# A transformer trunk on one core: G loads queued behind the weights, and part of the output added in memory by accumulating transfers

## The chip, the core and the metric

The kernel runs on one core of a Trainium2 chip. A core has five engines with instruction streams of their own: TensorE (PE, matmuls, with weight loads shown apart as PEld), VectorE (DVE), ScalarE (ACT), GpSimd (POOL) and SyncE (SP). Each stream is executed in order. SP, ACT and POOL also issue DMAs; those of SP and ACT go through hardware queues, those of POOL through a software queue, and all are carried out by the same 16 DMA engines. PE accumulates in PSUM; the other engines and the DMAs work on SBUF, the on-chip memory of 128 partitions. "Memory" below is the chip's large off-chip memory, in which inputs, outputs and spilled intermediates lie.

The metric is the device time of one execution in microseconds (us), as a median over runs.

## The reference

One layer over 512 tokens of width 2048, all in float32:

```python
h = rms_norm(x, g0)
P = h @ w_in                       # 11 column blocks for four groups of heads
mixed = concat[A, B, C, D] @ w_out # stick-breaking attention, differential attention, RG-LRU, gated conv
x = x + rms_norm(mixed, g1)        # this sum is x1
h = rms_norm(x, g2)
u = causal_dwconv(h @ ffn_w_up, ffn_conv_w)
g, up = split(u)
x = x + rms_norm((gelu(g) * up) @ ffn_w_down, g3)
```

An RMS norm multiplies each token by the inverse root of its mean square and each channel by a gain. The product gelu(g) * up is called G here; it has 4096 channels, 32 blocks of 128. The last line is where the change does most: the output is x1 plus the scaled result of the down projection.

## The kernel before

**Layout.** Channels lie on the partitions and the 512 tokens along the free axis. A matrix product is done in float32 precision by three passes on split operands: every operand is kept as a rounded high part and a remainder (hi and lo). ScalarE makes hi by a cast and VectorE makes lo by a subtraction (`split`, lines 175 to 182; for weights lines 99 and 100 in `chunk`, 1008 and 1009 in `operand`).

**Order.** PE's order is the order of the program text (`manual_schedule`, line 53). The other engines' orders are made by a planner, which picks among the instructions that are ready by priority: the place in the text, with loads and splits of weights far ahead (`high_priority`). `issue_after(ins)` puts an instruction behind another on the same engine's stream; it is an order only and no wait for the other to finish. Work that accompanies the matmuls is hung on a counter: `at(block, fn)` runs a function when the counter `clock[0]` reaches a step, and the loop of `group` counts four steps for each chunk of weights (`tick`, lines 111 to 114).

**First norm and residual.** After the out projection, for each half of the tokens, `residual(hf)` (line 828) scales the result and adds it onto x: half of it by VectorE (line 842), half by accumulating DMAs from POOL into SBUF (line 838). Then `squares` makes the squares (ScalarE, line 853) and their sum (VectorE, line 855) and stores x1 to memory (`x1_d`, line 859). `norm2` (line 861) sums over the partitions with four matmul passes (line 866), makes the inverse root and splits the normalized h. It is hung 40 steps behind `residual` (line 845).

**Up projection.** `seven` (line 1023) does seven block products in place of eight for each unit of 128 channels (a scheme of Strassen's kind); it needs sums of weight blocks, of which some are made by accumulating DMAs from POOL (line 1018). Each unit ends in a convolution (lines 948 and 950), and `glu` (line 957) stores one block of G to memory (`g_d`, line 959).

**Down projection.** G comes back from memory in pairs of blocks. `load_pair` (line 1128) takes a tile of the pool `ystage` (two tiles) and issues two loads of 256 KB from SP; `load_g` (line 1134) splits two pairs into a tile of four blocks. Blocks 0 to 3 (line 1142) and 20 to 31 (lines 1213 to 1215) are used by plain products, blocks 4 to 19 by the scheme of seven (`load_build`, line 1175, `down_unit`, line 1194). The plain products of blocks 20 to 31 come last: three groups of 512 output channels with all tokens, and the fourth once for each half of the tokens (lines 1243 to 1246).

**Last norm and output.** `SumSq` (line 789) takes the squares of the 16 output blocks. POOL adds the squares up in order, except for the last `direct` ones, which PE takes as further terms of its sum over the partitions (lines 811 and 812). `rstd_of` (line 184) makes the inverse root in six small instructions (lines 188 to 194) with two temporary tiles `f1`. `finish(hf)` (line 1229) does the rest for a half: for q = 0 to 3 it loads 4 blocks of x1 (512 KB, line 1235), multiplies the result by the inverse root (line 1239), adds x1 (line 1240) and stores pieces of two blocks (256 KB, line 1241), in turn from SP and ACT. The x1 of q = 0 has a pool of its own with one tile (`x1p`), that of q = 1 to 3 uses the two tiles of `ystage`. For the second half this whole sequence lies behind the last matmul of the kernel.

Of the kernel before, what the change touches and what calls it, by code (L numbers as in the profile page):

```python
# [9 lines left out]
F32 = mybir.dt.float32  # L10
F32R = mybir.dt.float32r
AF = mybir.ActivationFunctionType
ALU = mybir.AluOpType
# [3 lines left out]
P = 128  # L17
S = 512
# [30 lines left out]
def trunk(ctx: ExitStack, tc: tile.TileContext, xT, params, consts, wgate, w_in, w_out, w_up0, w_up, w_dn, w_dns, out):  # L49
    nc = tc.nc  # L50
    V, A, G, T = nc.vector, nc.scalar, nc.gpsimd, nc.tensor
# [9 lines left out]
    def mm_tile():  # L61
        return mm.tile([P, S], F32, name="mm")
# [23 lines left out]
    w_split, w_load = [], []  # L86
# [18 lines left out]
    clock = [0]  # L105

    def at(block, fn):
        assert block >= clock[0], (block, clock[0])
        beside.setdefault(block, []).append(fn)
# [62 lines left out]
    def repeated(t, n):  # L172
        return t.unsqueeze(1).broadcast_to([P, n, t.shape[-1]])

    def split(src, hi, lo, scale=None):
        if scale is None:
            A.copy(out=hi, in_=src)
            V.tensor_tensor(out=lo, in0=src, in1=hi.bitcast(F32), op=ALU.subtract)
        else:
            A.activation(out=hi, in_=src, func=AF.Copy, scale=scale)  # L180
            V.scalar_tensor_tensor(out=lo, in0=src, scalar=scale, in1=hi.bitcast(F32),
                                   op0=ALU.mult, op1=ALU.subtract)

    def rstd_of(ss, n, dst, tmp):

        w = dst.shape[-1]
        v = tmp()[:, 0:w]
        V.tensor_scalar(out=v, in0=ss, scalar1=-0.5 / n, scalar2=-0.5 * EPS, op0=ALU.mult, op1=ALU.add)
        y = tmp()[:, 0:w]
        A.activation(out=y, in_=ss, func=AF.Ln, scale=1.0 / n, bias=eps)  # L190
        exp = A.activation(out=y, in_=y, func=AF.Exp, scale=-0.5)
        V.tensor_tensor(out=v, in0=v, in1=y, op=ALU.mult)
        V.tensor_tensor(out=v, in0=v, in1=y, op=ALU.mult)
        V.scalar_tensor_tensor(out=dst, in0=v, scalar=1.5, in1=y, op0=ALU.add, op1=ALU.mult)
        return exp
# [23 lines left out]
    x1_d = [dram.tile([P, 2, 4, S // 2], F32, name=f"x1_d{q}") for q in range(4)]  # L219
    g_d = [dram.tile([P, S], F32, name=f"g_d{k}") for k in range(FF // P)]  # L220
# [4 lines left out]
    with ExitStack() as ph:  # L225
# [145 lines left out]
        for i in range(2):  # L371
            V.tensor_tensor(out=lmp[:, i * 64:(i + 1) * 64], in0=par[:, dl + 128 * i:dl + 128 * i + 64],
                            in1=par[:, dl + 128 * i + 64:dl + 128 * i + 128], op=ALU.mult)
# [247 lines left out]
        ys, vs = {}, []  # L621
# [150 lines left out]
    with ExitStack() as ph:  # L772
        wide = ph.enter_context(tc.tile_pool(name="wide", bufs=2))
        ystage = ph.enter_context(tc.tile_pool(name="ystage", bufs=2))
# [6 lines left out]
        ph2 = norm_ph.enter_context(tc.tile_pool(name="ph2", bufs=1))  # L781
# [2 lines left out]
            return t2p.tile([P, S], dt, name="f2")  # L784

        def t1(dt=F32):
            return ph2.tile([P, S // 2], dt, name="f1", bufs=3)

        class SumSq:

# [37 lines left out]
        def residual(hf):  # L828

            ts = HALVES[hf]  # L830
            ss1[hf].rstd(rstd1[:, ts])
            acc = ph2.tile([P, 2, S // 2], F32, name="s2")
            for q in range(4):
                for i in range(2):
                    m = mg[q][hf][:, 2 * i:2 * i + 2]
                    V.tensor_tensor(out=m, in0=m, in1=repeated(rstd1[:, ts], 2), op=ALU.mult)
                if q < 2:
                    G.dma_start(out=xs[q][hf], in_=mg[q][hf], accum_op=ALU.add)
            for q in range(2, 4):
                for i in range(2):  # L840
                    m, x = (t[q][hf][:, 2 * i:2 * i + 2] for t in (mg, xs))
                    V.tensor_tensor(out=x, in0=x, in1=m, op=ALU.add)
            for q in range(4):
                at(clock[0] + 20 + 3 * q, lambda q=q: squares(hf, q, acc))
            at(clock[0] + 40, lambda: norm2(hf, acc))

        def squares(hf, q, acc):

            with tc.issue_after(w_split[-1].ins):
                for i in range(2):  # L850
                    n = 2 * q + i
                    sq = acc if n == 0 else t2().rearrange("p (k t) -> p k t", k=2)
                    A.activation(out=sq, in_=xs[q][hf][:, 2 * i:2 * i + 2], func=AF.Square)
                    if n > 0:
                        V.tensor_tensor(out=acc, in0=acc, in1=sq, op=ALU.add)
                for i in range(4):
                    A.activation(out=mg[q][hf][:, i], in_=xs[q][hf][:, i], func=AF.Copy, scale=gain(2, 4 * q + i))
            with tc.issue_after(w_load[-1].ins):
                nc.sync.dma_start(out=x1_d[q][:, hf], in_=xs[q][hf])

        def norm2(hf, acc):

            ts = HALVES[hf]
            ps = mm_tile()[:, 0:S // 2]
            for i in range(2):
                T.matmul(ps, lhsT=ones, rhs=acc[:, i], start=i == 0, stop=i == 1)
            with tc.high_priority(offset=AHEAD):
                rstd_of(ps, D, rstd2[:, ts], t1)
            for k in range(0, KT, 2):
                ks = slice(k % 4, k % 4 + 2)  # L870
                h = mg[k // 4][hf][:, ks]
                V.tensor_tensor(out=h, in0=h, in1=repeated(rstd2[:, ts], 2), op=ALU.mult)
                split(h, actq[k // 4][:, 0, ks, ts], actq[k // 4][:, 1, ks, ts])
            if hf == 1:
                sums_of_h()
# [9 lines left out]
        def sums_of_h():  # L885


            t1_, t3_ = (wide.tile([P, 2, KT // 2, S // 2], F32R, name="xs") for _ in range(2))
            for i in range(2):
                h11, h12, h22 = mg[i][0], mg[i][1], mg[2 + i][1]  # L890
                ks = slice(4 * i, 4 * i + 4)
                V.tensor_tensor(out=h11, in0=h11, in1=h12, op=ALU.subtract)
                split(h11, t1_[:, 0, ks], t1_[:, 1, ks])
                V.tensor_tensor(out=h12, in0=h22, in1=h12, op=ALU.subtract)
                split(h12, t3_[:, 0, ks], t3_[:, 1, ks])
            for i in range(2):
                t1, h21, h22 = mg[i][0], mg[2 + i][0], mg[2 + i][1]
                V.scalar_tensor_tensor(out=h22, in0=t1, scalar=-1.0, in1=h22, op0=ALU.mult, op1=ALU.subtract)
                V.scalar_tensor_tensor(out=h21, in0=h22, scalar=-1.0, in1=h21, op0=ALU.mult, op1=ALU.subtract)
            t4_ = wide.tile([P, 2, KT // 2, S // 2], F32R, name="mg")  # L900
            for i in range(2):
                split(mg[2 + i][0], t4_[:, 0, 4 * i:4 * i + 4], t4_[:, 1, 4 * i:4 * i + 4])
            for n, t in (("T1", t1_), ("T3", t3_), ("T4", t4_)):
                tops[n] = [t[:, :, k] for k in range(8)]
# [219 lines left out]
        m3 = [m3p.tile([P, 4, S], F32, name=f"m3{q}") for q in range(4)]  # L1124
# [2 lines left out]

        def load_pair(k, pool=None):
            y = (ystage if pool is None else pool).tile([P, 2, S], F32, name="ys")
            for i in range(2):  # L1130
                nc.sync.dma_start(out=y[:, i], in_=g_d[k + i])
            return y

        def load_g(k, t):

            for i in range(0, 4, 2):
                with tc.high_priority(offset=AHEAD):
                    split(load_pair(k + i), t[:, 0, i:i + 2], t[:, 1, i:i + 2])
                for n in range(i, i + 2):
                    g_h[k + n], g_l[k + n] = t[:, 0, n], t[:, 1, n]  # L1140
# [69 lines left out]
        x1p = ph.enter_context(tc.tile_pool(name="x1p", bufs=1))  # L1210
        ph2 = ph.enter_context(tc.tile_pool(name="ph3", bufs=1))
        rstd3 = ph2.tile([P, S], F32, name="rstd3")
        load_g(20, wide.tile([P, 2, 4, S], F32R, name="xs"))
        load_g(24, wide.tile([P, 2, 4, S], F32R, name="xs"))
        load_g(28, act.tile([P, 2, 4, S], F32R, name="a1"))
        ss3 = [SumSq("q3", 3), SumSq("q3", 3)]

        def last_group(g, hfs, ts, pool_tile):
            def evac(u, ps):
# [9 lines left out]
        def finish(hf):  # L1229
            ts = HALVES[hf]  # L1230
            ss3[hf].rstd(rstd3[:, ts])
            for q in range(4):
                x1 = (x1p if q == 0 else ystage).tile([P, 2, S], F32, name="ys")
                x1 = x1.rearrange("p a (b t) -> p (a b) t", b=2)
                nc.sync.dma_start(out=x1, in_=x1_d[q][:, hf])
                for i in range(2):
                    ks = slice(2 * i, 2 * i + 2)
                    t, x = m3[q][:, ks, ts], x1[:, ks]
                    V.tensor_tensor(out=t, in0=t, in1=repeated(rstd3[:, ts], 2), op=ALU.mult)
                    V.tensor_tensor(out=x, in0=t, in1=x, op=ALU.add)  # L1240
                    (nc.scalar if i else nc.sync).dma_start(out=out[hf, 2 * q + i], in_=x)

        for g in range(3):
            last_group(g, (0, 1), ALL, mm_tile if g % 2 == 0 else pa_tile)
# [117 lines left out]
```

## Time and profile before

| | us |
|---|---|
| median of 3 runs | 1788.43 (1787.79 to 1792.69) |
| the profiled execution, its time | 1789.35 |
| the profiled execution, its span (first to last instruction) | 1787.7 |

The span is what the profile's times refer to, counted from its start. The mean TensorE clock granted in this execution was 0.990. The second part of the page cuts the span into 40 slices of 44.7 us; PE's digit is 7 to 9 in all of them but the last, where it is 4. The longest idle time of PE in front of one instruction is 10.1 us (the waits of line 1039), the sum of all its waits that the trace names is about 35 us.

How to read the lines that follow in the next parts: a timeline line has the start, the time from there to the end of the instructions merged in it, engine, line of the kernel, operation, the tile written and the tiles read, shapes and count, and in brackets how long the engine had been idle before and what ended that. SPq, ACTq and POOL lines with DMA_DIRECT2D are issues of DMAs; when the data lands is told by the view of DMAs, whose lines have the engine, count, size of one and the median time from issue to landing. A line of the DMA queues has packets, megabytes, and the share of the 16 engines' time that they took.

### The profile page before, as it was taken

How to read it: one execution, taken by the hardware profiler on the slowest of the kernel's cores; microseconds unless marked ns; L12 is line 12 of the kernel's file. 1: busy time of each engine (PE TensorE's matmuls, PEld its weight loads, DVE VectorE, ACT ScalarE, POOL GpSimd, SP SyncE). 2: the span in 40 equal slices, each digit the busy share in tenths (PEclk: the TensorE clock that was granted, in tenths of full speed). 3: DMA queues.
4: the chain of work that ended last, by engine and by line, in shares of the span. 5: the costliest groups of instructions: out<-in, count | busy, mean ns of one | idle time of the engine just before them, and what ended most of it. 6: DMA issues, size and time to landing. Idle time of an engine off the chain costs nothing.

```text
span 1787.7 us, 25033 instructions
## 1 busy us (share of the span) xinstructions
PE 1730.8 (97%) x9500; PEld 1501.8 (84%) x9500; DVE 1245.1 (70%) x1903; ACT 897.0 (50%) x1335; POOL 162.3 (9%) x230
## 2 busy tenths in 40 slices
PE   8999999999999999999799999999999999999994
PEld 7778788887888889999688888888888878888884
DVE  7885576666666324879788888888878886775336
ACT  6443676655334334767455555555555663334432
POOL 0000011100000111100011111111111001110211
PEclk9999999999999999999899999999999999999997
DMA  7234222242222535775788888888888669876235
GB/s 255 83 100 142 83 77 77 88 143 94 94 93 89 195 107 178 234 223 175 227 212 226 234 232 213 246 230 222 235 230 228 174 205 247 223 191 188 94 122 185
DMA packets 97024, 308.13 MB, mean 172 GB/s; under 512 B 10468, under 2 KB 14820, under 8 KB 96904
## 3 DMA queue, kind: packets, MB, share of 16 engines
q1 hardware_dynamic: 80056, 247.29, 41.8%
q0 software_dynamic: 15696, 57.15, 17.2%
q10 hardware_dynamic: 1152, 2.10, 0.3%
q8 instruction: 74, 1.21, 0.3%
q14 instruction: 46, 0.38, 0.1%
HBM read 265.59 MB, written 21.24 MB: 160 GB/s over the span
## 4 chain that ended last, share of the span: by engine, by line
PE 89%; DMA 4%; DVE 4%; ACT 2%; issue 1%; SPq 0%; DVEq 0%; ACTq 0%; POOLq 0%
PE mm L150 34%; PE mm L1039 25%; PE mm L1044 13%; PE pa L150 5%; PE mm L121 2%; PE mm L122 2%; PE mm L123 2%; PE pa L575 1%; DVE w_lo L100 1%; DMA a<-in_w_dns_dram 1%; DMA ys<-x_d 1%; DMA g_d<-f 1%; PE pa L123 1%; PE pa L121 1%; PE pa L122 1%
## 5 line engine op out<-in xcount | busy, mean ns | idle before, releaser
L100 DVE TENSOR_TENSOR w_lo<-w_raw,w_hi 128x1024 fp32r<-128x1024 f32 (+1 forms) x207 | 253.6, 1225 | 263.5 <-PE mm L150 136.1
L150 PE MATMUL mm<-a,w_hi 128*128 128x512 f32 (+1 forms) x1744 | 371.0, 363 | 2.7 <-DVE t L318 2.1
L99 ACT CAST w_hi<-w_raw 128x1024 fp32r<-128x1024 f32 (+1 forms) x207 | 216.1, 1045 | 293.3 <-PE mm L150 214.9
L150 PEld LDWEIGHTS mm<-a,w_hi 128*128 128x128 f32 x1744 | 296.7, 189 | 53.4 <-DVE t L318 2.6
L1039 PE MATMUL mm<-a,w_hi 128*128 128x512 f32 x1088 | 276.4, 396 | 16.3 <-DVE ub L1106 10.1
L1008 ACT CAST w_hi<-w_raw 128x1024 fp32r<-128x1024 f32 x145 | 152.2, 1050 | 203.5 <-PE mm L1039 175.6
L1039 PEld LDWEIGHTS mm<-a,w_hi 128*128 128x128 f32 x1088 | 197.8, 191 | 52.7 <-DVE ub L1106 10.3
L1009 DVE TENSOR_TENSOR w_lo<-w_raw,w_hi 128x1024 fp32r<-128x1024 f32 x145 | 177.0, 1221 | 36.9 <-ACT w_hi L1008 36.9
L150 PE MATMUL mm<-a,w_lo 128*128 128x512 f32 (+1 forms) x872 | 198.1, 366 | 0.0
L150 PEld LDWEIGHTS mm<-a,w_lo 128*128 128x128 f32 x872 | 147.2, 189 | 24.0 <-issue 1.5
L1044 PEld LDWEIGHTS mm<-a,w_lo 128*128 128x128 f32 x1088 | 150.5, 193 | 11.0
L1044 PE MATMUL mm<-a,w_lo 128*128 128x256 f32 x1088 | 153.5, 284 | 0.0
L1039 PE MATMUL mm<-xs,w_hi 128*128 128x512 f32 x576 | 144.3, 392 | 0.2 <-DVE ub L1106 0.2
L1008 ACT CAST w_hi<-mg 128x1024 fp32r<-128x1024 f32 x84 | 87.7, 1044 | 86.4 <-PE mm L1039 83.0
L1009 DVE TENSOR_TENSOR w_lo<-mg,w_hi 128x1024 fp32r<-128x1024 f32 x84 | 102.5, 1221 | 24.8 <-ACT w_hi L1008 24.8
L1039 PEld LDWEIGHTS mm<-xs,w_hi 128*128 128x128 f32 x576 | 103.6, 189 | 19.0 <-DVE ub L1106 0.4
L1039 PE MATMUL mm<-mg,w_hi 128*128 128x512 f32 x352 | 88.2, 392 | 0.8 <-DVE m L1200 0.8
L1044 PEld LDWEIGHTS mm<-xs,w_lo 128*128 128x128 f32 x576 | 78.6, 190 | 5.6
L1106 DVE TENSOR_TENSOR ub<-ub,mm 128x256 f32<-128x256 f32 x196 | 81.3, 415 | 0.7 <-ACT ub L1103 0.7
L1044 PE MATMUL mm<-xs,w_lo 128*128 128x256 f32 x576 | 80.3, 282 | 0.0
L150 PE MATMUL pa<-a,w_hi 128*128 128x256 f32 (+1 forms) x512 | 72.8, 294 | 2.9 <-ACT w_hi L99 2.9
L1039 PEld LDWEIGHTS mm<-mg,w_hi 128*128 128x128 f32 x352 | 63.3, 189 | 12.3 <-issue 1.0
(267 smaller groups left out, 2556.9 us busy)
## 6 DMA issues: line engine op xcount, KB each, us to landing
w_raw<-in_w_up_dram SPq DMA_DIRECT2D x115, 512.0 KB, 5.1
w_raw<-in_w_in_dram SPq DMA_DIRECT2D x87, 512.0 KB, 3.5
mg<-in_w_up_dram SPq DMA_DIRECT2D x56, 512.0 KB, 3.9
w_raw<-in_w_out_dram SPq DMA_DIRECT2D x48, 512.0 KB, 3.5
w_raw<-in_w_dn_dram SPq DMA_DIRECT2D x38, 512.0 KB, 3.6
w_raw<-mg POOLq DMA_DIRECT2D x28, 512.0 KB, 5.8
mg<-in_w_up_dram POOLq DMA_DIRECT2D x27, 512.0 KB, 7.9
w_raw<-in_w_up_dram POOLq DMA_DIRECT2D x27, 512.0 KB, 9.2
```

The source lines that it names most:

```text
L99: w_split.append(A.copy(out=hi[:, sl], in_=raw[:, sl]))
L100: V.tensor_tensor(out=lo[:, sl], in0=raw[:, sl], in1=hi[:, sl].bitcast(F32), op=ALU.subtract)
L121: T.matmul(ps, lhsT=sh, rhs=mh, start=first, stop=False)
L122: T.matmul(ps, lhsT=sh, rhs=ml, start=False, stop=False)
L123: T.matmul(ps, lhsT=sl, rhs=mh, start=False, stop=last)
L150: T.matmul(pss[u], lhsT=a, rhs=b, start=c == 0 and kk == 0 and not low and i == 0, stop=False)
L575: T.matmul(cum[:, o0:o0 + w], lhsT=stat, rhs=mv, start=n == 0, stop=n == len(todo) - 1)
L1008: w_split.append(A.copy(out=by4(hi), in_=v))
L1009: V.tensor_tensor(out=by4(lo), in0=v, in1=by4(hi).bitcast(F32), op=ALU.subtract)
L1039: T.matmul(ps.rearrange("p (a t) -> p a t", a=2), lhsT=hi[:, k * P:(k + 1) * P], rhs=tops[name][k], start=first and k == 0, stop=False, **kw)
L1044: T.matmul(ps[:, 0:256], lhsT=lo[:, k * P:(k + 1) * P], rhs=tops[name][k][:, 0], start=False, stop=k == 7, **kw)
L1106: V.tensor_tensor(out=t, in0=t, in1=ps[:, 256:512], op=ALU.add)
```

## The change

Four edits:

- `load_pair` issues its two loads behind the last weight load that stands ahead of it in the text (`issue_after(w_load[-1].ins)`).
- For the second half of the tokens, output pieces 0 to 4 of 8 take another way. Five copies from x1 in memory to the output in memory are issued from SP behind the weights of the last unit of the scheme of seven. In `finish(1)` the scaled result of each of these pieces is added onto the output in memory by an accumulating DMA from POOL. They need no x1 in SBUF and no add by VectorE. Pieces 5 to 7, and the whole first half, still load x1, add and store.
- The x1 of q = 0 and of q = 3 now use the tile of `x1p`, q = 1 and q = 2 the two tiles of `ystage`. For the second half only half of q = 2 is loaded, and q = 3.
- The last norm's sums take two squares directly instead of one, with four tiles for squares instead of three; the temporary tiles `f1` go from three to two; `norm2` is hung 43 steps behind `residual` for the first half and 41 for the second, instead of 40.

```diff
         def t1(dt=F32):
-            return ph2.tile([P, S // 2], dt, name="f1", bufs=3)
+            return ph2.tile([P, S // 2], dt, name="f1", bufs=2)
...
-            at(clock[0] + 40, lambda: norm2(hf, acc))
+            at(clock[0] + (43 if hf == 0 else 41), lambda: norm2(hf, acc))
...
             y = (ystage if pool is None else pool).tile([P, 2, S], F32, name="ys")
-            for i in range(2):
-                nc.sync.dma_start(out=y[:, i], in_=g_d[k + i])
+            with tc.issue_after(w_load[-1].ins):
+                for i in range(2):
+                    nc.sync.dma_start(out=y[:, i], in_=g_d[k + i])
             return y
...
-        ss3 = [SumSq("q3", 3), SumSq("q3", 3)]
+
+        IN_OUT = 5
+        with tc.issue_after(w_load[-1].ins):
+            for n in range(IN_OUT):
+                nc.sync.dma_start(out=out[1, n], in_=x1_d[n // 2][:, 1, 2 * (n % 2):2 * (n % 2) + 2])
+        ss3 = [SumSq("q3", 4, 2), SumSq("q3", 4, 2)]
...
         def finish(hf):
             ts = HALVES[hf]
             ss3[hf].rstd(rstd3[:, ts])
-            for q in range(4):
-                x1 = (x1p if q == 0 else ystage).tile([P, 2, S], F32, name="ys")
-                x1 = x1.rearrange("p a (b t) -> p (a b) t", b=2)
-                nc.sync.dma_start(out=x1, in_=x1_d[q][:, hf])
-                for i in range(2):
-                    ks = slice(2 * i, 2 * i + 2)
-                    t, x = m3[q][:, ks, ts], x1[:, ks]
-                    V.tensor_tensor(out=t, in0=t, in1=repeated(rstd3[:, ts], 2), op=ALU.mult)
-                    V.tensor_tensor(out=x, in0=t, in1=x, op=ALU.add)
-                    (nc.scalar if i else nc.sync).dma_start(out=out[hf, 2 * q + i], in_=x)
+            def scaled(n):
+                t = m3[n // 2][:, 2 * (n % 2):2 * (n % 2) + 2, ts]
+                V.tensor_tensor(out=t, in0=t, in1=repeated(rstd3[:, ts], 2), op=ALU.mult)
+                return t
+
+            n = 0
+            while hf == 1 and n < IN_OUT:
+
+                G.dma_start(out=out[hf, n], in_=scaled(n), accum_op=ALU.add)
+                n += 1
+            while n < 8:
+                q, i = n // 2, n % 2
+                if i == 0 or hf == 1 and n == IN_OUT:
+                    x1 = (x1p if q % 3 == 0 else ystage).tile([P, 2, S], F32, name="ys")
+                    x1 = x1.rearrange("p a (b t) -> p (a b) t", b=2)
+                    nc.sync.dma_start(out=x1[:, 2 * i:], in_=x1_d[q][:, hf, 2 * i:])
+                t, x = scaled(n), x1[:, 2 * i:2 * i + 2]
+                V.tensor_tensor(out=x, in0=t, in1=x, op=ALU.add)
+                (nc.scalar if i else nc.sync).dma_start(out=out[hf, n], in_=x)
+                n += 1
```

## The prediction

> **What bounds the kernel now.** I read the page first, then the chain of waits, then the timeline wherever the chain leaves TensorE, because only there can a change of loads, buffers and an output path move the end.
>
> ```profile
> span 1787.7 us, 25033 instructions
> PE 1730.8 (97%) x9500; PEld 1501.8 (84%) x9500; DVE 1245.1 (70%) x1903; ACT 897.0 (50%) x1335; POOL 162.3 (9%) x230
> ...
> q1 hardware_dynamic: 80056, 247.29, 41.8%
> q0 software_dynamic: 15696, 57.15, 17.2%
> ...
> PE 89%; DMA 4%; DVE 4%; ACT 2%; issue 1%; SPq 0%; DVEq 0%; ACTq 0%; POOLq 0%
> ```
>
> TensorE is busy 97% of the span and the chain is PE for 89% of it. The change removes no matmul. It can only win what lies in PE's holes, and in the tail after PE's last matmul. The tail is the largest hole. Its timeline:
>
> ```profile
> 1759.18 0.38 SPq L1235 DMA_DIRECT2D ys<-x_d  x1
> ...
> 1763.63 1.73 POOL L802 TENSOR_TENSOR ss<-ss,q 128x256 f32<-128x256 f32 x2 [0.21 <-ACT q L798]
> ...
> 1765.42 0.70 PE L812 MATMUL pa<-ss,con 128*128 128x256 f32 x2 [1.92 <-POOL ss L802]
> ...
> 1765.95 0.59 PE L812 MATMUL pa<-q,con 128*128 128x256 f32 x2
> 1768.01 0.69 DVE L1240 TENSOR_TENSOR ys<-m,ys 128x512 f32<-128x512 f32 x1 [3.70 <-DMA ys<-x_d]
> 1768.61 0.41 DVE L188 TENSOR_SCALAR f<-pa 128x256 f32<-128x256 f32 x1
> ...
> 1770.93 0.42 DVE L194 SCALAR_TENSOR_TENSOR rstd<-f,f 128x256 f32<-128x256 f32 x1
> 1771.39 1.29 DVE L1239 TENSOR_TENSOR m<-m,rstd 128x512 f32<-128x512 f32 x2
> ...
> 1772.60 1.28 DVE L1240 TENSOR_TENSOR ys<-m,ys 128x512 f32<-128x512 f32 x2
> ...
> 1782.97 1.29 DVE L1240 TENSOR_TENSOR ys<-m,ys 128x512 f32<-128x512 f32 x2 [3.07 <-DMA ys<-x_d]
> ```
>
> PE's last matmul ends at 1766.54, 21.2 us before the end. Two waits for x1 stand in that tail. The first half's last add (L1240) waits for its x1 until 1768.01, and the second half's L188 stands behind it on VectorE, 2.07 us after PE is done. From L188 to the end of rstd (1771.35) is 2.74. Then come 8 multiplies and 8 adds at 0.60 each, with a second wait of 3.07 for the last x1 tile, whose buffer came free late. The last store is issued at 1784.3:
>
> ```profile
> L1241 ACTq DMA_DIRECT2D out_dram<-ys x8: 338/338/377, 1756.9 to 1784.3; - x8
> ```
>
> **The tail after the change.** PE first. One more square per half goes straight to PE (direct 1 to 2). A term costs PE 0.53 (1765.42 to 1765.95), so the first half's sum puts up to 0.53 into the matmul stream. In the second half POOL does one add less (1.73/2 = 0.87), and the sum is done at 1766.54 - 0.87 + 0.53 = 1766.20. Together the end of PE work is 1766.7, level with before.
>
> The first half's last x1 (q = 3) changes its buffer: it now goes into x1p, which is free at 1759.18 (there before loads the second half's first x1). With the 4.6 of such a load (row below) it lands at 1763.8, both adds are over by 1765.2 and L188 follows PE at once, at 1766.8. rstd is done at 1769.5, 1.85 earlier. If that load comes late, the 1.85 shrinks.
>
> Now the output. The 5 accumulating pieces need a multiply and no add on VectorE, and no x1 in SBUF; pieces 5 to 7 keep both. Multiply 0 ends at 1770.2. POOL then issues five DMAs, and the prices of an accumulating DMA are these (window 862 to 868, where that queue was alone, and all of L1018):
>
> ```profile
> q0 software_dynamic: 221, 0.84, 79.1%
> ```
>
> ```profile
> L1018 POOL DMA_DIRECT2D w_raw<-in_w_up_dram x27: 862/865/888, 875.6 to 1396.0; - x27
> ...
> DMA to landing us min/median/max: 4.5/7.8/10.8
> ```
>
> ```profile
> ys<-x_d SPq DMA_DIRECT2D x8, 512.0 KB, 4.6
> ```
>
> ```profile
> out_dram<-ys ACTq DMA_DIRECT2D x1, 256.0 KB, 2.1
> ```
>
> The last row is the last store of all (window 1780 to 1788). Issue is 0.87 each, so the first bytes move at 1771.1 and the fifth issue begins near 1773.9. The rate: 0.84 MB in 79.1% of 6 us is 177 GB/s alone, and 57.15 MB in 17.2% of 1787.7 is 186 GB/s over the whole run (plain transfers: 247.29 MB in 41.8%, 331 GB/s). Five pieces of 262144 bytes are 1.31 MB, 7.05 us at 186. The quickest landing of 512 KB, 4.5, is 0.87 of issue, 2.8 of transfer and 0.8 of rest. So the fifth lands at 1771.1 + 7.05 + 0.8 = 1778.95 if the DMA engines serve nothing else. The three plain stores and one x1 load (1.31 MB, 4.0 us at 331) share the time: 1782.95 at worst. I take the middle, 1781.0. No row has an accumulation whose destination is memory; all of before's go to SBUF. So this is a choice by the nearest rows, and both ends go into the range: 1775.9 (five at the plain 331 GB/s, 4.0) and 1787 (half the rate, with the x1 load beside it).
>
> Nothing is queued behind the five on POOL, whose last own work is the sum of squares. On SP the load of the last x1 waits for the first half's last stores, issued near 1765.2 and landed 2.1 later; it is in by 1772, its first add comes near 1774. Behind it stands only piece 6's store. VectorE is not late: 8 multiplies and 3 adds at 0.60 end at 1776.2, and the last plain store lands 2.1 later, at 1778.3. Before, the end stood 1787.7 - (1784.3 + 2.1) = 1.3 behind the last landing. So the tail ends at 1781.0 + 1.3 = 1782.3, **5.4 earlier** (bounds: 8.1, where the plain store ends last, and -0.6).
>
> The Trainium skill (DMA: Bandwidth & Descriptors, Anatomy of one DMA — SWDGE (gpsimd) path) puts a DMA from POOL at about 2.0 us plus its bytes over 436 GB/s, an estimate of 2.6 for 256 KB and 3.2 for 512 KB. By that the accumulations are in by 1776.5 and the plain stores end last (a rival below). The trace speaks against it for accumulations: none of 512 KB lands in under 4.5. The same section says that completion waits for the written memory's receipt, heaviest for HBM; that speaks for the slow rivals, and no run here shows it yet.
>
> **The later norm2.**
>
> ```profile
> 745.79 1.13 PE L866 MATMUL mm<-s,con 128*128 128x256 f32 x4 [1.77 <-DVE s L855]
> ...
> 748.67 2.08 PE L150 MATMUL pa<-a,w_hi 128*128 128x256 f32 x16
> ...
> 751.55 2.08 PE L150 MATMUL pa<-a,w_hi 128*128 128x256 f32 x16
> ...
> 754.45 1.28 DVE L178 TENSOR_TENSOR a<-mg,a 128x512 fp32r<-128x512 f32 x2
> ...
> 760.20 2.08 PE L150 MATMUL mm<-a,w_hi 128*128 128x256 f32 x16
> ```
>
> ```profile
> 797.97 1.13 PE L866 MATMUL mm<-s,con 128*128 128x256 f32 x4 [0.31 <-DVE s L855]
> ```
>
> PE stands 1.77 and 0.31 at L866, since the squares' sum is not ready. A chunk of this half-width loop takes 2.88 (748.67 to 751.55) in four steps of the clock, 0.72 each. Three steps are 2.16 of other matmuls, more than 1.77; one step is more than 0.31. Both waits go, 2.08. Next to be late are the splits of h: L866 runs at 745.79 - 1.77 + 2.16 = 746.18, 0.4 later than now, and the first split, ready at 755.1, is used at 760.20 less 1.77, so 2.9 of cover is left. As VectorE's chain starts 0.4 later in each half, I take **1.7** (bounds 0 and 2.08). f1 with two buffers costs nothing: an rstd takes two and is done before the next begins.
>
> **The tied loads.** Only loads that ran ahead of weights move: G 0 to 3 and the pairs 20 and 22.
>
> ```profile
> 873.36 0.47 SPq L959 DMA_DIRECT2D g_d<-f  x1
> ...
> 883.95 0.33 SPq L1131 DMA_DIRECT2D ys<-g_d  x1
> 883.96 0.72 ACT L948 ACTIVATE f<-ub,par 128x512 f32<-128x512 f32 x1 [7.28 <-DMA g_d<-f]
> ...
> 886.64 3.78 PE L1039 MATMUL mm<-a,w_hi 128*128 128x512 f32 x8 [10.14 <-DVE ub L1106]
> ...
> 891.72 1.99 PE L1039 MATMUL mm<-mg,w_hi 128*128 128x512 f32 x8
> ...
> 894.50 2.00 PE L1039 MATMUL mm<-a,w_hi 128*128 128x512 f32 x8
> ```
>
> ```profile
> 1393.33 3.12 SPq L1002 DMA_DIRECT2D w_raw<-in_w_up_dram  x2
> ...
> 1458.60 0.80 SPq L1131 DMA_DIRECT2D ys<-g_d  x2
> ...
> 1483.49 0.90 SPq L1131 DMA_DIRECT2D ys<-g_d  x2
> ```
>
> ```profile
> 1597.16 5.91 SPq L1002 DMA_DIRECT2D w_raw<-in_w_dns_dram  x3
> ```
>
> ```profile
> 1411.50 1.05 ACT L177 CAST a<-ys 128x1024 fp32r<-128x1024 f32 x1
> ```
>
> ```profile
> 1612.38 2.00 ACT L177 CAST xs<-ys 128x1024 fp32r<-128x1024 f32 x2
> ```
>
> ```profile
> 876.00:886.00 10.00, 0.50 (x5) 0.30 (x3) 5.53 (x10) 1.66 (x3) 0.52 (x1) 0.76 0.86 229
> ```
>
> Here is PE's longest hole, 10.14, and the first G load stands in it: SP is blocked on it until 883.95. It is tempting to book the hole to it. But ACT's L948 starts at 883.96 because the same store of g_d, issued at 873.36, ahead of the load, lands then and frees its buffer. The store takes 10.6 to land because the DMA engines are 0.86 busy there (row below) with the weights and accumulations issued before it, not because of the G load behind it. So I take **0** for the tie here; the hole and the slow product after it (5.08 from 886.64 to 891.72) stay. The loads' new places: G 0 to 3 after the last up weight, about 1396.5, needed at 1411.50; pairs 20 and 22 and the five copies in memory after 1603.1, needed from 1612.38. Each has 9 us or more, against the 4.6 of a load of 512 KB. The cover is PE's matmuls; if a weight slips behind the 2.36 MB at 1603 (7.1 us at 331 GB/s) I put it at up to 3 us.
>
> **Sum.** 5.4 + 1.7 + 0 = 7.1. In the profiled execution's own terms the span falls from 1787.7 to 1780.6 and its time from 1789.35 to 1782.3; that execution lies 0.92 above the median 1788.43, so I predict **1781.3**. The likeliest case's own range is 1777.5 to 1785.5.
>
> **The rivals.**
> *The hole at 876 goes after all* (0.2). For it: SP is free, and ACT's L948 would find another f buffer free sooner if the order around it moves. Against it: the store stands ahead of the load. Worth 10.14 plus 5.08 less the usual step of 2.78 (891.72 to 894.50), 12.4: 1768.9.
> *An accumulation costs no more than a plain store* (0.12). Then VectorE's 11 steps and the last plain store set the end: 8.1 + 1.7: 1778.6. For it: the software queue's rows are taken beside weights. Against it: 177 GB/s with the queue alone.
> *Accumulating into memory runs at half the rate* (0.12): 14.1 instead of 7.05, the tail gains nothing and norm2 alone is left: 1786.7, no change.
> *It runs at a quarter, and the kernel is slower than before* (0.06). Mechanism: the DMA engine reads and rewrites its destination in memory, on the one software queue, where nothing hides it. 28.2 us: 1771.1 + 28.2 + 0.8 + 1.3 = 1801.4, less 1.7 is 12.0 above 1787.7: 1800.4. It decides from 81 GB/s down (16.2 us). For it: no row shows such a destination. Against it: the 186 GB/s hold many accumulations whose source is memory (27 of them in the L1018 row).
> *The tie makes weights late* (0.07): PE waits near 1610 for 3 us: 1784.3.
>
> **Chances.** A measurement of this kernel can tell about 0.3%, 5.4 us: faster is below 1783.1, slower above 1793.8. The forecast's own case has 0.43, some 0.31 of it below 1783.1; with the hole (0.2), the cheap accumulation (0.12) and a share of the late weights (0.02) faster is 0.65; same is 0.12 + 0.12 + 0.05 = 0.29; slower 0.06. For 8 in 10 the range takes in most of the hole's case and the half-rate case: 1767 to 1787.
>
> **What would show it.** Right: no wait of PE at L866; L188 within 0.5 us of PE's last L812; no DVE wait for x1 in the tail; five POOL issues and a last landing near 1781 less 1.7; 10 us of PE idle still before the fifth unit. Wrong: that hole gone or moved; accumulations landing over 8 us after issue; L1131 or the copies ahead of a weight that PE waits for.

## The result: slower, by 0.46%

| | before | after |
|---|---|---|
| median, us | 1788.11 (1786.48 to 1792.69, 4 runs) | 1797.05 (1795.8 to 1798.69, 4 runs) |
| profiled execution: time, span | 1789.35, 1787.7 | 1795.8, 1793.8 |
| last matmul ends | 1766.54 | 1766.32 |
| second half's inverse root ends | 1771.35 | 1769.10 |
| from there to the end of the span | 16.35 | 24.7 |

The ratio is 1.0046, 95% interval 1.003 to 1.0062. The prediction was 1781.3, with a range from 1767 to 1787, and it was wrong in sign. The table places the loss: TensorE is done as early as before, the inverse root is done 2.25 earlier, and then 8.35 more pass until the end.

Line numbers of the changed kernel, where they differ: accumulation onto the output 1246, multiply 1240, add 1255, x1 load 1253, plain store 1256, copies of x1 to the output 1221, loads of G 1132, taking of the scheme's products 1201.

The top of the page of the changed kernel:

```profile
span 1793.8 us, 25042 instructions
...
PE 1729.7 (96%) x9504; PEld 1500.7 (84%) x9504; DVE 1242.8 (69%) x1898; ACT 896.0 (50%) x1335; POOL 166.2 (9%) x233
...
q1 hardware_dynamic: 80056, 246.50, 41.2%
q0 software_dynamic: 17056, 58.47, 17.8%
...
PE 87%; issue 4%; DMA 3%; DVE 3%; ACT 2%; POOL 0%; POOLq 0%; SPq 0%; ACTq 0%; DVEq 0%
```

One row points at the cause: the software queue (q0) has 1360 packets more than before (15696) for 1.31 MB more: 272 for each of the five new DMAs. The 109 accumulations of before have 15696 / 109 = 144 each, for twice the bytes. A piece of the result lies in SBUF as two runs of 1 KB in each of 128 partitions, so it makes 256 packets and 16 small ones.

The last row has to be read with care. In the chain "issue", time in which an engine waited for nothing that the profile can name, has grown from 1% to 4%. Only 13.8 us of it, 0.8% of the span, lie between the five accumulations (the timeline below), and the page of e1, which is much faster, has 4% too. So this share is no measure of the loss; the timeline is.

The tail after, as timeline (PE, VectorE and POOL):

```profile
1764.75 0.70 PE L812 MATMUL pa<-ss,con 128*128 128x256 f32 x2 [1.75 <-POOL ss L802]
1765.29 1.03 PE L812 MATMUL pa<-q,con 128*128 128x256 f32 x4
1766.36 0.42 DVE L188 TENSOR_SCALAR f<-pa 128x256 f32<-128x256 f32 x1 [1.11 <-PE pa L812]
...
1768.68 0.42 DVE L194 SCALAR_TENSOR_TENSOR rstd<-f,f 128x256 f32<-128x256 f32 x1
1769.14 4.30 DVE L1240 TENSOR_TENSOR m<-m,rstd 128x512 f32<-128x512 f32 x7
...
1770.29 1.13 POOL L1246 DMA_DIRECT2D out_dram<-m  x1 [5.59 <-DVE m L1240]
1774.79 1.09 POOL L1246 DMA_DIRECT2D out_dram<-m  x1 [3.37 <-DVE ys L1255]
1779.60 1.09 POOL L1246 DMA_DIRECT2D out_dram<-m  x1 [3.72 <-issue]
1784.09 1.09 POOL L1246 DMA_DIRECT2D out_dram<-m  x1 [3.40 <-issue]
1788.53 1.08 POOL L1246 DMA_DIRECT2D out_dram<-m  x1 [3.34 <-issue]
```

The seven multiplies that stand first, the five of these pieces among them, are over at 1773.4, yet POOL issues the five DMAs 4.4 to 4.8 apart and stands idle for 3.3 to 3.7 between them. The view of line 1246 has the other half of the picture:

```profile
  issue: 10.5, 3
...
DMA to landing us min/median/max: 4.1/4.2/4.5
```

Each DMA lands about 4.2 after its issue begins, and the next issue begins some 0.3 later: 1779.60 + 4.2 = 1783.8, then 1784.09. One is in flight at a time. (The second row names an add of VectorE as releaser, but its piece had been multiplied long before. The add is only the last event that the profile saw on a semaphore. VectorE as a whole is done at 1775.97, and three of the four pauses lie behind that.) The rate is the second thing. In the window from 1788 to 1794 the fifth is alone on the DMA engines:

```profile
DMA packets 272, 0.26 MB, mean 44 GB/s; under 512 B 16, under 2 KB 272, under 8 KB 272
...
q0 software_dynamic: 272, 0.26, 36.4%
```

36.4% of 6 us is 2.18 us of all 16 engines for 262144 bytes, 120 GB/s. The last lands at 1788.53 + 4.1 = 1792.6, and the span ends 1.2 later.

### The profile page after: what moved, and what is told of

Same layout as the page of the kernel before. It is cut to its first block, busy times and chain, and to the rows that moved or that the text cites. A ratio compares the mean times of both kernels' runs of the same rounds, so it can differ in the third digit from the quotient of the medians.

```text
span 1793.8 us, 25042 instructions
## 1 busy us (share of the span) xinstructions
PE 1729.7 (96%) x9504; PEld 1500.7 (84%) x9504; DVE 1242.8 (69%) x1898; ACT 896.0 (50%) x1335; POOL 166.2 (9%) x233
## 3 DMA queue, kind: packets, MB, share of 16 engines
HBM read 265.59 MB, written 22.55 MB: 161 GB/s over the span
## 4 chain that ended last, share of the span: by engine, by line
PE 87%; issue 4%; DMA 3%; DVE 3%; ACT 2%; POOL 0%; POOLq 0%; SPq 0%; ACTq 0%; DVEq 0%
PE mm L150 33%; PE mm L1039 24%; PE mm L1044 13%; PE pa L150 5%; PE mm L121 2%; PE mm L123 2%; PE mm L122 2%; PE pa L575 1%; DMA xs<-mg 1%; DMA a<-in_w_dns_dram 1%; DVE w_lo L100 1%; DMA g_d<-f 1%; PE pa L680 0%; PE pa L122 0%; PE pa L121 0%
## 5 line engine op out<-in xcount | busy, mean ns | idle before, releaser
L1009 DVE TENSOR_TENSOR w_lo<-w_raw,w_hi 128x1024 fp32r<-128x1024 f32 x145 | 177.0, 1221 | 38.2 <-ACT w_hi L1008 37.7
L1044 PEld LDWEIGHTS mm<-a,w_lo 128*128 128x128 f32 x1088 | 149.3, 191 | 10.8
```

The source lines that it names most:

```text
L1009: V.tensor_tensor(out=by4(lo), in0=v, in1=by4(hi).bitcast(F32), op=ALU.subtract)
L1044: T.matmul(ps[:, 0:256], lhsT=lo[:, k * P:(k + 1) * P], rhs=tops[name][k][:, 0], start=False, stop=k == 7, **kw)
```

## The experiments

Unless the text says otherwise, each kernel is the changed one with the edit that is shown. For the tail one number is compared, from the end of the second half's inverse root (line 194) to the end of the span, since what happens ahead of it varies by some us from one execution to the next (26 runs of before beside e3, e5, e6 and e8 lie between 1784.84 and 1794.21):

| kernel | root ends | span ends | tail | median (runs) | ratio to before, 95% |
|---|---|---|---|---|---|
| before | 1771.35 | 1787.7 | 16.35 | 1788.11 (4) | |
| after | 1769.10 | 1793.8 | 24.7 | 1797.05 (4) | 1.0046 (1.003 to 1.0062) |
| e1 contiguous pieces | 1767.95 | 1782.4 | 14.45 | 1784.45 (8) | 0.9978 (0.9968 to 0.9988) |
| e2 more room | 1767.08 | 1782.6 | 15.5 | 1784.6 (1) | |
| e4 no accumulation | 1767.38 | 1787.2 | 19.8 | 1790.48 (10) | 1.0017 (1.0004 to 1.0029) |
| e7 loads not tied | 1770.09 | 1796.1 | 26.0 | 1797.87 (1) | |
| e3 three pieces | 1771.24 | 1788.3 | 17.1 | 1786.08 (10) | 0.9991 (0.998 to 1.0002) |
| e5 x1 ahead | 1770.58 | 1783.8 | 13.2 | 1783.69 (10) | 0.9979 (0.9967 to 0.9992) |
| e6 value tiles | 1766.60 | 1781.1 | 14.5 | 1780.85 (5) | 0.9962 (0.9949 to 0.9975) |
| e8 norm2 at 40 | 1768.96 | 1783.8 | 14.8 | 1785.73 (10) | 0.9986 (0.9976 to 0.9995) |
| h1 three, x1 ahead | 1763.54 | 1777.1 | 13.6 | 1776.77 (5) | 0.9938 (0.9924 to 0.9952) |
| h2 five, x1 ahead | 1765.25 | 1779.9 | 14.65 | 1779.19 (5) | 0.9956 (0.9943 to 0.9969) |
| h3 none, x1 ahead | 1759.91 | 1773.4 | 13.5 | 1775.16 (5) | 0.9938 (0.9923 to 0.9953) |

The median of before beside these runs was 1788.33 (e1, e2, e4, e7), 1787.7 (e3, e5, e6, e8) and 1788.09 (h1 to h3). The kernels e6 and h1 to h3 have other line numbers behind line 943, the others behind their own first edit.

### e1: the same five accumulations from contiguous pieces

```diff
             n = 0
+            if hf == 1:
+                flat_t = act.tile([P, 8, 2, S // 2], F32, name="a2")
             while hf == 1 and n < IN_OUT:
-                G.dma_start(out=out[hf, n], in_=scaled(n), accum_op=ALU.add)
+                t = m3[n // 2][:, 2 * (n % 2):2 * (n % 2) + 2, ts]
+                V.tensor_tensor(out=flat_t[:, n], in0=t, in1=repeated(rstd3[:, ts], 2), op=ALU.mult)
+                G.dma_start(out=out[hf, n], in_=flat_t[:, n], accum_op=ALU.add)
```

> The scaled result of pieces 0 to 4 is written into a tile of its own, so that one partition's share of a piece is one run of 2 KB in SBUF instead of two of 1 KB; nothing else is changed. Theory 'room': the software queue has room for the descriptors of one DMA of 272 packets only, so each waits for the landing of the one before. With 144 packets, like the accumulations of before, two or three fit: the first three issues stand about 1.1 us apart, the others wait for one landing; last landing near 1780, span 1781 to 1783 where the changed kernel had 1793.8. Theory 'memory': an accumulation whose destination is memory runs one at a time whatever its shape: the issues stay 4.5 us apart and the span stays at 1793 to 1794.

POOL in the tail of e1, and the software queue in its page:

```profile
1769.10 2.71 POOL L1250 DMA_DIRECT2D out_dram<-a  x3 [5.55 <-DVE a L1249]
1773.65 0.87 POOL L1250 DMA_DIRECT2D out_dram<-a  x1 [1.85 <-DVE ys L1259]
1775.77 0.86 POOL L1250 DMA_DIRECT2D out_dram<-a  x1 [1.25 <-DVE ys L1259]
```

```profile
q0 software_dynamic: 16416, 58.47, 17.9%
```

The bytes, the destination and the operation are those of the change; only the number of packets is less, 720 / 5 = 144. Now three are issued without a pause; the fourth waits until the first has landed (1769.10 + 4.2 = 1773.3) and the tail is 10 us shorter. So an accumulation into memory does not run one at a time whatever its shape, and the theory 'memory' falls.

### e2: the same packets, more room for descriptors

```diff
-    nc = bacc.Bacc("TRN2", target_bir_lowering=False, num_devices=1, dynamic_dma_scratch_size=1024)
+    nc = bacc.Bacc("TRN2", target_bir_lowering=False, num_devices=1, dynamic_dma_scratch_size=2048)
...
-                    x1 = (x1p if q % 3 == 0 else ystage).tile([P, 2, S], F32, name="ys")
+                    x1 = (act.tile([P, 2, S], F32, name="a3") if q % 3 == 0 else ystage.tile([P, 2, S], F32, name="ys"))
```

(The second edit makes the space for the first: the x1 tile of `x1p` moves into a tile that is free by then.)

> The space set aside for the software queue's descriptors goes from 1024 to 2048; to make room for it the tile of x1p is taken from a tile that is free at that time. The five DMAs keep their shape. Theory 'room': three of 272 packets are now in flight, first issues about 1.1 us apart, span 1781 to 1784. Theory 'memory': 4.5 us apart as before, span 1793 to 1794.

```profile
1768.19 3.35 POOL L1245 DMA_DIRECT2D out_dram<-m  x3 [5.52 <-DVE m L1239]
1772.87 1.08 POOL L1245 DMA_DIRECT2D out_dram<-m  x1 [1.32 <-DVE a L1254]
1775.42 1.08 POOL L1245 DMA_DIRECT2D out_dram<-m  x1 [1.47 <-issue]
```

This is POOL's timeline of e2. With 272 packets as in the change, but twice the space, three are issued back to back, and the fourth waits for the first to land (4.4 later). So the wait that the profile calls "issue" is a wait for room in the software queue. 1024 bytes held one DMA of 272 packets or three of 144 (so 432 fit and 544 don't); 2048 bytes held three of 272.

The Trainium skill (DMA: Bandwidth & Descriptors, SWDGE vs HWDGE vs iDMA) says that GpSimd writes the descriptors of its DMAs into rings in a reserved part of SBUF, and the size table of SBUF — State Buffer puts that at 16 KiB per partition; this kernel reserves 1 KiB. e2 fits that: with twice the space three DMAs are in flight in place of one. That the issuing engine stands still while there is no room is what these runs add.

### e4: no accumulation, all other edits kept

```diff
-        IN_OUT = 5
+        IN_OUT = 0
```

> No piece is accumulated and no copy in memory made; all other edits stay. Both theories: the tail is 8 multiplies and 8 adds with one wait left, for the x1 of q = 3, whose one tile is free only when the stores of q = 0 have landed. PE ends near 1766.3, rstd near 1769.1, last x1 near 1779.5, span near 1784, some 3 to 4 us less than before (1787.7) and 9 to 10 less than the changed kernel. If the loss of the change lay ahead of the tail, the span would stay above 1790.

VectorE in the tail of e4:

```profile
1774.68 1.29 DVE L1255 TENSOR_TENSOR ys<-m,ys 128x512 f32<-128x512 f32 x2 [3.56 <-DMA ys<-x_d]
...
1782.55 1.29 DVE L1255 TENSOR_TENSOR ys<-m,ys 128x512 f32<-128x512 f32 x2 [2.96 <-DMA ys<-x_d]
```

e4 was forecast to gain and did not: two adds wait for x1 in place of one, 6.5 in all. SP issues the last two loads of x1 only at 1770.08 and 1778.56. Both go into the one tile of `x1p`, which q = 0 and q = 3 now share, and each waits until the stores from that tile have landed: first those of the first half's last pieces, then those of the second half's own first pieces. Without the accumulations the other edits together, the new use of the tiles among them, gain nothing (1.0017), and the accumulations on top of them cost another 1797.05 - 1790.48 = 6.6.

### e7: loads of G not tied

```diff
-            with tc.issue_after(w_load[-1].ins):
-                for i in range(2):
-                    nc.sync.dma_start(out=y[:, i], in_=g_d[k + i])
+            for i in range(2):
+                nc.sync.dma_start(out=y[:, i], in_=g_d[k + i])
```

> The loads of G are not tied, the rest of the change stays. My step that the tie is worth nothing: the hole of PE near 876 is there as in both kernels (10 to 13 us), PE's last matmul ends within 1.5 us of the changed kernel's 1766.3, the span is 1792 to 1796. Rival: the tie is worth something either way: PE's end moves by more than 1.5 us.

The hole ahead of the fifth unit, on PE, first in e7 and then in the changed kernel with ScalarE's line 948:

```profile
884.62 3.78 PE L1039 MATMUL mm<-a,w_hi 128*128 128x512 f32 x8 [10.78 <-DVE ub L935]
```

```profile
880.58 0.72 ACT L948 ACTIVATE f<-ub,par 128x512 f32<-128x512 f32 x1 [8.72 <-DMA g_d<-f]
...
884.46 3.56 PE L1039 MATMUL mm<-a,w_hi 128*128 128x512 f32 x8 [12.78 <-DVE ub L935]
```

The product starts at the same time with the loads tied or not, and 1797.87 against 1797.05 is within the spread of single runs. In the changed kernel no load of G stands near 876 any more (in e7 the first is issued at 880.73), and the hole is there in both: as the prediction had it, it hangs on the store of G's first block, for whose buffer ScalarE waits 8.72.

### e6: e1, and tiles of their own for two gated products

```diff
-        def conv(t, half, unit, minus=False):
+        def conv(t, half, unit, minus=False, y=None):
...
-            y = t2()
+            y = t2() if y is None else y
...
-                y = conv(ub[half, u], half, u)
+                own = half == 1 and u < 2
+                y = conv(ub[half, u], half, u, y=ystage.tile([P, 2, S], F32, name="ys")[:, 0] if own else None)
```

> As e1, and the gated products of units 0 and 1 get tiles of their own (the staging tiles for the G loads, idle at that time since these loads are tied behind the weights), so that ScalarE's line 948 no longer waits for the store of unit 0 to land. Theory of the prediction (the hole on TensorE at 876 comes from that wait of 8.7 us on ScalarE): the hole of 10 to 13 us shrinks by 4 to 11 and the slow restart goes, so 1773 to 1780 against 1784.45 of e1. Rival (the weights of that stretch are late anyway, behind the stores and loads on the same 16 engines): the hole becomes a wait for a weight and less than 2 us are gained, 1783 or more.

The same place in e6:

```profile
880.02 3.78 PE L1040 MATMUL mm<-a,w_hi 128*128 128x512 f32 x8 [6.95 <-DVE ub L1107]
```

The hole is 6.95 in place of 12.78 (12.38 in e1) and the median falls by 3.6 against e1, to 1780.85, just short of the band that was expected. ScalarE no longer waits for the store. What is left is VectorE: from 870.9 to 881.4 it works without a pause, mostly on the convolutions and gated products of the last plain units, and the add that frees PE's accumulator (879.55) stands behind most of them. The slow restart, which was expected to go, stays: from this product to the next it is 5.05 (880.02 to 885.07). The tiles that e6 uses are idle there only because the loads of G are tied (before, the first of them was issued at 883.95); without the tie it wasn't tried.

### e8: e1, with norm2 at 40 steps

```diff
-            at(clock[0] + (43 if hf == 0 else 41), lambda: norm2(hf, acc))
+            at(clock[0] + 40, lambda: norm2(hf, acc))
```

> As e1, with norm2 hung 40 steps behind the residual for both halves as before the change. Theory of the prediction (the later norm2 is worth 1.7 us on TensorE and all of it reaches the end): 1786.2 against 1784.45 of e1. Rival (the gain of 3 us by 860 is lost again where the sums of weights in memory set the pace, near 1466 to 1486): no difference, 1784.5.

PE in e8, then in the changed kernel:

```profile
745.91 1.13 PE L866 MATMUL mm<-s,con 128*128 128x256 f32 x4 [1.77 <-DVE s L855]
796.71 1.13 PE L866 MATMUL mm<-s,con 128*128 128x256 f32 x4 [0.31 <-DVE s L855]
```

```profile
744.31 1.13 PE L866 MATMUL mm<-s,con 128*128 128x256 f32 x4
796.09 1.13 PE L866 MATMUL mm<-s,con 128*128 128x256 f32 x4 [1.08 <-DVE s L855]
```

With 43 steps the first wait is gone. The second is not: it grows from 0.31 to 1.08, though its matmuls stand one step later. From one and the same wait of PE near 664 to its first product of the scheme (857.17 - 666.10 in e1, 857.18 - 664.38 in e8) PE needs 191.07 against 192.80, so the later norm2 is worth 1.73 there. The medians differ by 1.28 the same way, but the two intervals overlap: that it reaches the end in full is not settled.

### e5 and e3: what the waits for x1 and the number of pieces are worth

e5 sets `IN_OUT` to 0 and loads the second half's x1 ahead:

```diff
+        x1b = act.tile([P, KT, S // 2], F32, name="a2")
         with tc.issue_after(w_load[-1].ins):
-            for n in range(IN_OUT):
-                nc.sync.dma_start(out=out[1, n], in_=x1_d[n // 2][:, 1, 2 * (n % 2):2 * (n % 2) + 2])
+            for q in range(4):
+                nc.sync.dma_start(out=x1b[:, 4 * q:4 * q + 4], in_=x1_d[q][:, 1])
...
-                if i == 0 or hf == 1 and n == IN_OUT:
+                if hf == 1:
+                    x1 = x1b[:, 4 * q:4 * q + 4]
+                elif i == 0:
```

> No accumulation at all: the x1 of the whole second half is loaded behind the last weights into a tile that is free by then, so that no addition waits for a load. It tells what the waits for x1 alone are worth. If they are all that holds the tail of before, VectorE does 16 instructions of 0.65 to 0.69 without a pause, 10.7 us behind an inverse root that ends at about 1767.5, and the last store lands 2 to 3 later: about 1783, as e1 (1784.45) and 5 less than before. If the plain stores are the limit, it stays at 1788 to 1790 as without accumulations (e4, 1790.48).

The tail is 13.2: no add waits, VectorE runs its 16 instructions from 1770.61 to 1780.3 and the last store follows. This simplest way has the shortest tail of all, and is as fast as e1 with its five accumulations.

e3 is e1 with `IN_OUT = 3`.

> As e1 (scaled pieces in contiguous tiles, so 144 packets for each accumulating DMA), with three pieces added in memory in place of five. Theory 'room' (the software queue holds three DMAs of 144 packets at a time and POOL waits for the first to land before it issues a fourth): the three are issued one right behind another, 0.87 each, are in flight together and land by about 1776; VectorE then sets the end: 8 multiplies and 5 additions at 0.65 behind the inverse root are 8.4 us, so the last store is issued near 1776 and the run takes about 1782, 2 less than e1 (1784.45). Theory 'latency' (an accumulation is late whatever lies before it in the queue): the third lands as late as the fifth of e1 and nothing is gained: 1784.5.

e3 told the theories apart only in part. POOL did issue the three without a pause (2.71 for three), but five plain pieces need more x1 than e1's three, and one add waited 5.50 for it. SP and VectorE in e3:

```profile
1774.74 0.32 SPq L1257 DMA_DIRECT2D ys<-x_d  x1
```

```profile
1782.88 0.69 DVE L1259 TENSOR_TENSOR ys<-m,ys 128x512 f32<-128x512 f32 x1 [5.50 <-DMA ys<-x_d]
```

This load took 8.0 to land, with the three accumulations in flight beside it, where such loads took 4.6 before. So the time says nothing of the room in the queue, and the wait is probably in part the accumulations' doing. That case is tested next.

### h1, h2, h3: three, five and no pieces, with x1 ahead and e6's tiles

h3 is e5 with the edit of e6. h1 and h2 are e6 with `IN_OUT` 3 and 5, and x1 of the other pieces loaded ahead into the tile `a3`:

```diff
+            x1b = act.tile([P, KT, S // 2], F32, name="a3")
+            for q in range(IN_OUT // 2, 4):
+                lo = 2 * max(0, IN_OUT - 2 * q)
+                nc.sync.dma_start(out=x1b[:, 4 * q + lo:4 * q + 4], in_=x1_d[q][:, 1, lo:])
```

> As e6 (contiguous pieces, tiles of their own for two gated products), three pieces added in memory, and the x1 of the other five pieces loaded behind the last weights into a free tile, so that the wait of 5.5 us for x1 that spoiled e3 is gone. From the end of the inverse root to the end of the span: 14.45 in e1 (five pieces), 13.2 in e5 (none). Theory 'room': three DMAs of 144 packets fit in the software queue at once, so POOL waits for nothing and VectorE's 8 multiplies and 5 additions (7.9 us) set the end: 11.3, which is 3 less than e6, so 1777.7. Theory 'latency' (each accumulation that finds others in flight lands late, room or not): 14 again, 1780.9 as e6.

> As h1 with five pieces added in memory: VectorE has 2 instructions less, but the fourth and fifth accumulation wait for room in the queue as in e1 (issued 4.5 and 6.7 us behind the first). Theory 'room': they set the end as in e1 and e6, 14.5 behind the inverse root, 1780.9, so 3 more than h1. If what held e1 was VectorE or the x1 of the plain pieces: as h1 or below, 1777.

> As h1 with nothing added in memory: x1 of all eight pieces loaded ahead (e5) and the tiles for two gated products (e6). VectorE's 16 instructions set the end, 13.2 behind the inverse root as in e5: 1779.6, that is 2 more than h1 and 1 less than h2 by theory 'room'. If the accumulations are worth nothing even with room: the same as h1.

h2 behaved as 'room' says in its tail (the fourth and fifth issue wait, 14.65), though its time lies halfway between the two forecasts. h1 did not: POOL waited for nothing between its three, VectorE was done at 1771.6, 8.1 behind the root, near the 7.9 that were reckoned, and still the tail is 13.6 in place of 11.3, no better than h3's 13.5. The windows of two us tell why (columns: length, POOL's busy time, clock, DMA share with 1 for all 16 engines busy, GB/s). h1:

```profile
1766.00:1768.00 2.00, 1.38 (x2) 0.50 1.00 121
1768.00:1770.00 2.00, 0.00 (x0) 0.50 1.11 194
1770.00:1772.00 2.00, 0.00 (x0) 0.50 1.07 304
1772.00:1774.00 2.00, 0.00 (x0) 0.50 1.02 389
```

h3:

```profile
1764.00:1766.00 2.00, 0.00 (x0) 0.50 0.49 183
1766.00:1768.00 2.00, 0.00 (x0) 0.50 0.49 182
1768.00:1770.00 2.00, 0.00 (x0) 0.50 0.49 183
```

With plain stores the engines are half busy and move 183 GB/s, 373 GB/s at full use. In h1 they are full from 1766 to 1774 and begin at 121 GB/s: the accumulations keep all 16 engines busy, and the plain stores land late beside them. The view of the store's line, cut to the tail, has the landings, of h1 and then of h3:

```profile
L1267 ACTq DMA_DIRECT2D out_dram<-a x3: 338/338/339, 1767.3 to 1771.6; - x3
...
DMA to landing us min/median/max: 3.8/5.2/5.7
```

```profile
L1260 ACTq DMA_DIRECT2D out_dram<-a x4: 338/338/339, 1762.5 to 1769.7; - x4
...
DMA to landing us min/median/max: 2.0/2.1/2.1
```

So VectorE saves three adds (it is done 8.1 behind the root in place of 9.8 in h3), and the DMA engines take it back. Neither of the two theories had this; 'latency' came nearest in the number, without the reason. h1 and h3 beat both kernels: h3, which adds nothing in memory, ran in 1775.16, 0.62% less than before (ratio 0.9938, 0.9923 to 0.9953). That is 4.4 below its forecast, with a tail near the forecast 13.2. The surplus lies ahead of the tail, where the root of h3 ends 3.6 earlier than that of h1; its cause stays open.

## Why the prediction was wrong, by its steps

**The step that failed** is "Issue is 0.87 each, so the first bytes move at 1771.1 and the fifth issue begins near 1773.9", with the term behind it, "Five pieces of 262144 bytes are 1.31 MB, 7.05 us at 186". From the first issue to the fifth landing the prediction had 1770.2 to 1781.0, 10.8. It was 1770.29 to 1792.6, 22.3. Two things were taken over from the accumulations of before that don't hold for these:

- *That they overlap.* The rows of before have DMAs of 144 packets, of which three fit in the queue. A piece of this change has 272 (and takes 1.09 to issue, not 0.87), and the queue holds one. e2, a single run, gives the price: with room for three and the same packets, it is 1768.19 to about 1781.3 (the end of its span less 1.3), 13.1. So 9.2 of the 11.5 that were missing are the lost overlap. No rival had it.
- *That 186 GB/s hold.* That was a mean over DMAs of 512 KB with 3.6 KB a packet. With 1 KB a packet and memory as destination it is 120 GB/s, 2.18 for a piece, 10.9 for five. That is 3.85 more than 7.05, and part of it was covered by the 2.05 that the prediction had put on top for sharing; the other 2.3 of the 11.5 lie here. How much of the lower rate comes from the smaller packets and how much from the destination no run separates.

By the last landing, 1792.6 against 1779.3 (1781.0 less 1.7): 11.5 from here, 1.8 because the first issue came later than the 1768.5 that norm2's gain would have given.

**The rival on the slow side** (quarter rate, 1800.4) came near the time with the wrong mechanism. It was to decide from 81 GB/s; the transfers themselves ran at 120, and only the pauses brought the whole down to 1.31 MB in 22.3, 59 GB/s. By engine time the half-rate rival was the closer one. The chance of 0.06 for slower rested on the rate alone and left out that a queue can be full. For the same reason its sign, accumulations landing over 8 after their issue, did not show: each landed within 4.5, and what was late were the issues.

**The Trainium skill's price** (DMA: Bandwidth & Descriptors, Anatomy of one DMA — SWDGE (gpsimd) path: 2.0 us plus bytes over 436 GB/s, by which we estimate 2.6 for a piece) does not fit here: a piece alone lands after 4.1 to 4.5, and its transfer takes 2.18 where the formula has 0.6.

**The rest of the tail was right.** L188 follows PE's last matmul by 0.04, the root ends 2.74 later, no add waits for x1, and VectorE's last add ends at 1775.97.

**PE's end** was to come 1.7 earlier by norm2 and came 0.22 earlier. On the way PE was ahead by more than that: line 1039's product behind the hole starts at 888.80 in place of 891.72, and the first down product at 1463.53 in place of 1466.42. Not all of it is norm2: e8, with norm2 at 40 steps, has the product behind the hole at 889.65, and in the changed kernel one of the two waits at line 866 stayed, at 1.08. The lead shrank where PE waits for sums of weight blocks:

```profile
1480.53 2.88 PE L1039 MATMUL mm<-a,w_hi 128*128 128x512 f32 x8 [4.21 <-DVE m L1201]
...
1484.92 2.02 PE L1039 MATMUL mm<-mg,w_hi 128*128 128x512 f32 x8
```

The product of the second row started at 1486.44 before, so 1.5 of 2.9 is left. (The wait of 4.21 ends with line 1201, which stands on VectorE behind the split of such a sum; the accumulating DMA that makes the sum took from 1468.20 to 1476.18.) At the first plain product behind the scheme it is 0.93 (1629.06 against 1629.99), and in the last norm's sums, where PE now takes two squares itself for each half instead of one (their products take 1.03 in place of 0.59), it falls to 0.22. The waits near 1470 and 1480 differ from one execution to the next (1.89 and 1.63 in e1, 1.45 and 3.82 in e8, a single one of 3.36 in h1), so how much of an early gain survives there is partly a matter of the execution.

**The tie at 0** was right, with its reason: the hole stayed, it hangs on the store and not on the load (e7, e6). So were the loads' new places; no weight is late behind them. SP in the changed kernel:

```profile
1393.61 2.67 SPq L1132 DMA_DIRECT2D ys<-g_d  x4
...
1601.62 2.55 SPq L1132 DMA_DIRECT2D ys<-g_d  x4
1604.21 4.40 SPq L1221 DMA_DIRECT2D out_dram<-x_d  x5
```

## What to carry to other kernels

Before a DMA from the software queue is put on the path that sets the end, count its packets (the contiguous runs of both sides), not only its bytes, and see how many such DMAs the queue's space holds; in these traces a full queue shows as idle time of POOL between issues, put down to "issue" or to an event that has nothing to do with it, and with one DMA in flight the pitch is one landing. Work that is moved off a compute engine onto accumulating transfers is paid in DMA engine time, so see what else those engines have to carry at that moment. Where an add waits for an operand, loading it ahead into a tile that has become free may be worth more than taking the add away.

## What the hardware showed that was not expected

- An accumulation into memory keeps all 16 engines busy for 2.18 us per 256 KB (120 GB/s), against 373 GB/s at full use for the plain stores of h3. With 2 KB a packet and company on the engines it was faster: in e1 from 1769 to 1782 the five took 63.6% of 13 us, 159 GB/s.
- The page's count of memory traffic shows no read of the destination: 265.59 MB are read before and after, and 1.31 MB more are written than before (21.24), which is the five copies. The row of the changed kernel:

```profile
HBM read 265.59 MB, written 22.55 MB: 161 GB/s over the span
```
